# SwiGLU and down projection of a hybrid decoder layer: seven block products in place of eight

## The chip, the cores and the metric

The kernel runs on one NeuronCore of a Trainium2 chip. The metric is the time of one execution on the device in microseconds. TensorE (PE) multiplies matrices and adds up in PSUM; VectorE (DVE), ScalarE (ACT) and GpSimd (POOL) do the elementwise work, the last of them on SBUF alone; SyncE (SP) issues most DMA transfers. Each engine works through its own list of instructions in order and waits on semaphores for the others.

## The reference, cut to what matters

One layer of a decoder trunk over 520 tokens (512 of a prompt, 8 single decode steps), 1024 features wide, all in float32. Two attention mixers come first; the change leaves them alone. Then:

```python
x = x + m @ w_o
gu = _rmsnorm(x, norm2_g) @ w_gu                                     # 1024 -> 2 x 2816
y = x + (jax.nn.silu(gu[..., :D_FF]) * gu[..., D_FF:]) @ w_down      # 2816 -> 1024
```

A last RMSNorm follows. The results are y and the windows of keys and values.

## The kernel before

Activations lie with features on the 128 partitions and tokens along the free axis: 8 chunks of 128 features, each 520 wide, cut in two halves of 256 and 264 tokens. A float32 product is made from three fast ones: each operand is split into a rounded part `hi` and a rest `lo`, and every product is hi·hi + hi·lo + lo·hi, all three into one PSUM bank. So one 128 x 128 block of weights against one half of the tokens is three matmuls (lines 245, 246, 248).

**Weights** come as jobs in a fixed list. SP loads a block of 128 x 1024 values (`raw`, 512 KB); ACT copies it rounded to `whi` (line 137) and DVE subtracts to get `wlo` (line 138). `weights` runs this one job ahead, with three raw buffers.

**SwiGLU** (lines 1152 to 1182): 22 chunks of 128 gated features. A chunk is 8 x 3 x 2 matmuls for the gate, into `psg`, and as many for the up part, into `psu`, so 96. `gated` then takes the SiLU on ACT, multiplies on DVE, copies rounded on ACT and subtracts on DVE: all 22 chunks stay in SBUF as `g_hi` and `g_lo`. The first two chunks run half by half, because the second half of the norm is still being made.

**Down projection** (lines 1264 on): 8 chunks of 128 output features, each 22 x 3 x 2 = 132 matmuls into `psd`, whose bank DVE adds to the residual `x2`. Each finished chunk is transposed to tokens, squared and multiplied with the final gain (`finish`); `emit_last` does the last chunk, the roots and the writes.

GpSimd has next to nothing to do in these two stages. It works in the earlier ones, where it multiplies projections with the rotary tables (lines 387, 428) beside DVE. The order of instructions on each engine is settled when the kernel is built, by the framework's scheduler, which starts from the order of the code; it may move an instruction ahead of others on its engine where no data stand against it. Buffers are waited for as the pools hand them out.

## Time and profile before

| | |
|---|---|
| median of 3 runs (lowest, highest) | 911.19 us (909.94, 915.88) |
| span of the profiled execution | 910.4 us, mean granted clock 0.991 |
| PE busy | 883.6 us, 97% of the span |
| DVE, ACT, POOL busy | 453.2, 340.4, 138.8 us |
| last matmul of the down projection starts | 900.61 us |

The profiled execution's own time is its span, 910.4 us; it lies 0.8 us under the median. The page gives the busy time of each engine, the span in 40 slices, the DMA queues, the chain of work that ended last, and the costliest groups of instructions. A busy PE counts matmuls that overlap in its pipeline, so a matmul's price is read from how many start in a window, not from the duration of one. In a timeline a row is start, duration, engine, line, operation and tiles.

### The profile page before, as it was taken

The numbers are of one execution on the slowest core, as the hardware profiler recorded it, in microseconds if no ns is written. First come the engines' busy times: TensorE is split into PE (matmuls) and PEld (weight loads), VectorE is DVE, ScalarE is ACT, GpSimd is POOL, SyncE is SP. The second block draws the span as 40 slices with busy tenths as digits, with TensorE's granted clock in tenths as the row PEclk, the third lists the DMA queues.
The fourth block names the chain that finished last, engine by engine and source line by source line (L and its number), as shares of the span: only waits on it lengthen the run. The fifth ranks groups of instructions, "written<-read, shape, count | busy, mean of one in ns | idle before, by whom it ended". The sixth has DMA issues, their size and how long they took to land.

```text
span 910.4 us, 17130 instructions
## 1 busy us (share of the span) xinstructions
PE 883.6 (97%) x7104; PEld 833.4 (92%) x7104; DVE 453.2 (50%) x920; ACT 340.4 (37%) x750; POOL 138.8 (15%) x114
## 2 busy tenths in 40 slices
PE   6998989999999999999999999999999999999996
PEld 6898889878998788779999999999999999999995
DVE  4878648754597554724464653333333333233322
ACT  6324324444466655533233443222222222222222
POOL 2335553423232112100000200000000000000000
PEclk9999999999999999999999999999999999999998
DMA  9546745331332211488568339357356555657302
GB/s 298 174 129 189 216 147 181 100 99 47 94 117 94 72 32 60 124 195 233 157 208 272 93 114 278 113 184 229 114 177 194 155 167 174 194 162 235 90 19 95
DMA packets 149854, 137.09 MB, mean 151 GB/s; under 512 B 5344, under 2 KB 144768, under 8 KB 148368
## 3 DMA queue, kind: packets, MB, share of 16 engines
q1 hardware_dynamic: 145472, 83.65, 33.0%
q10 hardware_dynamic: 2592, 46.08, 14.7%
q0 software_dynamic: 1712, 6.26, 2.1%
q8 instruction: 56, 0.92, 0.4%
q14 instruction: 22, 0.18, 0.1%
HBM read 129.14 MB, written 51.86 MB: 199 GB/s over the span
## 4 chain that ended last, share of the span: by engine, by line
PE 83%; DMA 6%; DVE 5%; issue 3%; POOL 2%; ACT 1%; SPq 0%; POOLq 0%; DVEq 0%; ACTq 0%
PE psu L246 5%; PE psu L248 5%; PE psg L248 5%; PE psu L245 5%; PE psg L246 5%; PE psg L245 5%; PE psd L245 4%; PE psd L248 4%; PE psd L246 4%; PE poa L931 3%; DMA raw_wo<-in_w_o 2%; DMA qc<-q_dram 2%; PE psgb L248 2%; PE psgb L245 2%; PE psgb L246 2%
## 5 line engine op out<-in xcount | busy, mean ns | idle before, releaser
L245 PE MATMUL psd<-g_hi,whi_wd 128*128 128x256 f32 (+1 forms) x352 | 93.4, 285 | 0.5 <-DVE x L1266 0.5
L246 PE MATMUL psd<-g_lo,whi_wd 128*128 128x256 f32 (+1 forms) x352 | 93.1, 282 | 0.0
L246 PE MATMUL psu<-h_lo,whi_wu 128*128 128x256 f32 (+1 forms) x352 | 93.0, 283 | 0.0
L246 PE MATMUL psg<-h_lo,whi_wg 128*128 128x256 f32 (+1 forms) x352 | 92.6, 282 | 0.0
L245 PE MATMUL psu<-h_hi,whi_wu 128*128 128x256 f32 (+1 forms) x352 | 92.1, 282 | 0.0
L245 PE MATMUL psg<-h_hi,whi_wg 128*128 128x256 f32 (+1 forms) x352 | 91.6, 282 | 0.0
L248 PE MATMUL psd<-g_hi,wlo_wd 128*128 128x256 f32 (+1 forms) x352 | 74.5, 283 | 0.0
L248 PE MATMUL psu<-h_hi,wlo_wu 128*128 128x256 f32 (+1 forms) x352 | 73.5, 283 | 0.0
L248 PE MATMUL psg<-h_hi,wlo_wg 128*128 128x256 f32 (+1 forms) x352 | 73.4, 282 | 0.0
L245 PEld LDWEIGHTS psd<-g_hi,whi_wd 128*128 128x128 f32 x352 | 66.3, 188 | 0.8 <-DVE x L1266 0.7
L245 PEld LDWEIGHTS psu<-h_hi,whi_wu 128*128 128x128 f32 x352 | 66.3, 188 | 0.0
L246 PEld LDWEIGHTS psd<-g_lo,whi_wd 128*128 128x128 f32 x352 | 66.2, 188 | 0.0
L245 PEld LDWEIGHTS psg<-h_hi,whi_wg 128*128 128x128 f32 x352 | 66.1, 188 | 0.0
L246 PEld LDWEIGHTS psu<-h_lo,whi_wu 128*128 128x128 f32 x352 | 66.1, 188 | 0.0
L246 PEld LDWEIGHTS psg<-h_lo,whi_wg 128*128 128x128 f32 x352 | 66.1, 188 | 0.0
L138 DVE TENSOR_TENSOR wlo_wg<-raw_wg,whi_wg 128x1024 fp32r<-128x1024 f32 x22 | 27.0, 1225 | 74.4 <-ACT whi_wg L137 69.8
L248 PEld LDWEIGHTS psd<-g_hi,wlo_wd 128*128 128x128 f32 x352 | 55.9, 188 | 0.0
L138 DVE TENSOR_TENSOR wlo_wd<-raw_wd,whi_wd 128x1024 fp32r<-128x1024 f32 (+1 forms) x24 | 27.3, 1137 | 57.1 <-ACT whi_wd L137 56.2
L248 PEld LDWEIGHTS psu<-h_hi,wlo_wu 128*128 128x128 f32 x352 | 55.6, 188 | 0.0
L248 PEld LDWEIGHTS psg<-h_hi,wlo_wg 128*128 128x128 f32 x352 | 55.6, 188 | 0.0
L137 ACT ACTIVATE whi_wd<-raw_wd 128x1024 fp32r<-128x1024 f32 (+1 forms) x24 | 23.7, 989 | 84.6 <-PE psd L246 67.9
L1156 DVE TENSOR_TENSOR sg<-sg,psu 128x256 f32<-128x256 f32 (+1 forms) x44 | 16.9, 421 | 72.5 <-PE psu L248 72.5
(371 smaller groups left out, 2465.6 us busy)
## 6 DMA issues: line engine op xcount, KB each, us to landing
raw_wg<-in_w_gu SPq DMA_DIRECT2D x22, 512.0 KB, 3.9
raw_wu<-in_w_gu SPq DMA_DIRECT2D x22, 512.0 KB, 5.3
raw_wd<-in_w_down SPq DMA_DIRECT2D x16, 512.0 KB, 5.5
out<-in_cache_b_kv ACTq DMA_DIRECT2D x8, 1022.0 KB, 5.5
out<-in_cache_b_kv ACTq DMA_DIRECT2D x8, 512.0 KB, 4.0
raw_qa<-in_w_in SPq DMA_DIRECT2D x8, 512.0 KB, 3.8
raw_ga<-in_w_in SPq DMA_DIRECT2D x8, 512.0 KB, 4.8
raw_gb<-in_w_in SPq DMA_DIRECT2D x8, 512.0 KB, 3.9
```

The source lines that it names most:

```text
L137: a = nc.scalar.activation(hi[:, :kc], raw[:, :kc], AF.Copy)
L138: nc.vector.tensor_tensor(lo[:, :kc], raw[:, :kc], hi[:, :kc].bitcast(F32), op=ALU.subtract)
L245: nc.tensor.matmul(ps[i], hi[:, k], xh[:, k0 + k, sl], start=st, stop=False)
L246: nc.tensor.matmul(ps[i], hi[:, k], xl[:, k0 + k, sl], start=False, stop=False)
L248: last_mm[0] = nc.tensor.matmul(ps[i], lo[:, k], xh[:, k0 + k, sl], start=False, stop=en).ins
L931: nc.tensor.matmul(po[64 * kv:64 * kv + 64, :], va[:, j - 1 + r, 64 * kv:64 * kv + 64], pts_[kv, r], start=(r == rel[0]), stop=(r == 1), s ...
L1156: nc.vector.tensor_tensor(sg, sg, pu, op=ALU.mult)
```

## The change

The last two stages become 2 x 2 block products in the form with seven multiplications (Strassen's, with Winograd's sums). Tokens are cut into two halves of 260. Feature chunks go in pairs, an even and an odd one, so the normalised input has four quarters (`hq`, split as `hb_hi`/`hb_lo`), and four sums of quarters are made and split once (`ht_hi`/`ht_lo`, in `sums`). A unit of kind "h" makes the gate and the up part of one chunk of gated features: its 2 x 2 block of weights is gate and up against even and odd. A unit of kind "d" makes two chunks of the output from one group of gated features. Each unit runs seven products q1 to q7 of four pairs each (three in the last group), with three matmuls a pair.

The sums of weight blocks are made on GpSimd in `prepare` (`s`, and `a21` in place), each of the seven operands is split by ACT and DVE as before, and the results are put together from four PSUM tiles (`a`, `e`, `f`, `b`) by DVE, ACT and GpSimd in `run`, `gated` and `down`. Operands are prepared four steps ahead (`NLA`). The first two chunks stay as they were, in `classical`.

Gated features no longer stay for all 22 chunks. Each pair is split, with its sums, as soon as it is made (`split_pair`), and the down projection takes them in three groups of 4, 4 and 3 pairs; so the order is chunks 0 to 8, down 0, chunks 9 to 16, down 1, chunks 17 to 21, down 2. `x2` gathers the three. The output projection and the norm before it get the same halves of 260. Counted from 0, the chunk of the output finished last is number 6, not 7, and `emit_last` and `emit_part` follow that.

On VectorE, the list of two SwiGLU chunks read before (`sg` the gated product, `g_lo` its rest, `wlo_wu` and `wlo_wd` rests of weights):

```order
L1156 TENSOR_TENSOR sg_8273<-sg_8273,psu_8161 128x256
L1156 TENSOR_TENSOR sg_8278<-sg_8278,psu_8162 128x264
L138 TENSOR_TENSOR wlo_wu_8411<-raw_wu_0_8286,whi_wu_8410 128x1024
L1158 TENSOR_TENSOR g_lo<-sg_8273,g_hi 128x256
L1158 TENSOR_TENSOR g_lo<-sg_8278,g_hi 128x264
```

and VectorE's list around units 11 to 13 now (`wlo_u..` rests of operands, `su` a weight sum, `zu` and `zsu` the working tiles of the combination, `psb`, `psa`, `psf` PSUM, `t`, `gb_lo`, `gt_lo` sums and rests of a pair of gated chunks):

```order
L1332 TENSOR_TENSOR zu_7993<-psb_u_8052,zsu_7992 128x260
L1301 TENSOR_TENSOR wlo_u13q_8091<-su_8085,whi_u13q_8090 128x512
L1348 TENSOR_TENSOR zu_7863<-psa_u_7861,zu_7863 128x260
L1301 TENSOR_TENSOR wlo_u13q_8048<-raw_u_7967,whi_u13q_8047 128x512
L1341 TENSOR_TENSOR zsu_7992<-psb_u_8052,zsu_7992 128x260
L1301 TENSOR_TENSOR wlo_u13q_8048<-su_7945,whi_u13q_8047 128x512
L1342 TENSOR_TENSOR zu_7993<-zsu_7992,psa_u_7991 128x260
L1220 TENSOR_TENSOR t_8029<-gq_7730,t_8029 128x260
L1343 TENSOR_TENSOR zsu_7992<-zsu_7992,psf_u_8071 128x260
L1254 TENSOR_TENSOR gb_lo_7751<-gq_7730,gb_hi_7750 128x3x260
```

Two whole-block subtractions per chunk have become seven of half a block, between them the five that read a PSUM bank and those for the pair of gated chunks.

On GpSimd, this is all that its list held before from the norm to the end (`rt`, `fst` and `fpart` are roots, `yts` the final gain):

```order
L1130 TENSOR_TENSOR h_lo<-h2f_5682,h_hi 128x256
L1118 TENSOR_TENSOR rt_5839<-rt_5839,nhalf 128x3
L1186 DMA yts<-in_final_norm_g 128x1024
L1227 TENSOR_TENSOR fst_9880<-fst_9880,nhalf 128x2
L1255 TENSOR_TENSOR fpart<-fpart,nhalf 128x3
```

and this is its list now around units 9 to 12 (`su` and `raw_u` weight sums, `gq` gated chunks, `t` their sums):

```order
L1289 TENSOR_TENSOR su_7669<-su_7669,raw_u_7562 128x512
L1346 TENSOR_TENSOR gq_6936<-gq_6936,zsu_7587 128x260
L1286 TENSOR_TENSOR su_7813<-su_7812,raw_u_7690 128x512
L1350 TENSOR_TENSOR gq_6936<-gq_6936,zu_7588 128x260
L1220 TENSOR_TENSOR t_7756<-gq_6936 128x260
L1285 TENSOR_TENSOR su_7944<-raw_u_7838 128x512
L1289 TENSOR_TENSOR su_7813<-su_7813,raw_u_7690 128x512
L1220 TENSOR_TENSOR t_7756<-gq_6936,t_7756 128x260
L1287 TENSOR_TENSOR raw_u_7838<-raw_u_7836,raw_u_7838 128x4x128
```

An engine that had no elementwise work in these stages now has seven instructions in each unit, all of them reading and writing SBUF.

The diff, cut to its core:

```diff
+NCL = 2
+NLA = 4
+STEP_RATE = 0.2
...
-    for i in range(NF):
+    for i in range(NCL):
         jobs.append((f"wg{i}", NK, [load_plain(cols_of(w_gu[0], P * i), NK)], split_plain))
-        jobs.append((f"wu{i}", NK, [load_plain(cols_of(w_gu[0], DFF + P * i), NK)], split_ff))
-    for i in range(NK):
-        for k0 in (0, 8, 16):
-            kc = min(8, NF - k0)
-            jobs.append((f"wd{i}_{k0}", kc, [load_plain(w_down[0, k0 * P:(k0 + kc) * P, P * i:P * i + P], kc)], split_ff if (i * 3 + k0 // 8) % 2 else split_plain))
+        jobs.append((f"wu{i}", NK, [load_plain(cols_of(w_gu[0], DFF + P * i), NK)], split_cl))
...
+    QOF = {(0, 0): 0, (1, 0): 1, (1, 1): 2, (0, 1): 3}
+    hq = op2.tile([P, 4, 4, HH], F32, tag="opT", name="hq")
+    hb_hi = hm.tile([P, 4, 4, HH], F32R, tag="hm", name="hb_hi")
+    hb_lo = hm.tile([P, 4, 4, HH], F32R, tag="hm", name="hb_lo")
+    pools["cl"] = op2.tile([P, 2 * NCL, NK, P], F32R, tag="opT", name="wcl")
...
+            q, i = QOF[m % 2, h], m // 2
+            nc.vector.scalar_tensor_tensor(hq[:, q, i], x2[:, m, sl], g2[:, m:m + 1], bc, op0=ALU.mult, op1=ALU.mult)
+            nc.scalar.activation(hb_hi[:, q, i], hq[:, q, i], AF.Copy)
+            (nc.gpsimd if h == 0 and m % 2 else nc.vector).tensor_tensor(hb_lo[:, q, i], hq[:, q, i], hb_hi[:, q, i].bitcast(F32), op=ALU.subtract)
...
-    def gated(m, h, pg, pu):
-        sl = slice(*SPAN[h])
-        sg = work.tile([P, HT], F32, tag="z", name=f"sg{m}{h}")[:, :SPAN[h][1] - SPAN[h][0]]
-        nc.scalar.activation(sg, pg, AF.Silu)
-        nc.vector.tensor_tensor(sg, sg, pu, op=ALU.mult)
-        nc.scalar.activation(g_hi[:, m, sl], sg, AF.Copy)
-        nc.vector.tensor_tensor(g_lo[:, m, sl], sg, g_hi[:, m, sl].bitcast(F32), op=ALU.subtract)
...
-    for m in range(2, NF):
-        pgs, pus = pair(f"psg{m}", "m"), pair(f"psu{m}", "b")
-        project(pgs, weights(f"wg{m}"), NK, h2_hi, h2_lo)
-        project(pus, weights(f"wu{m}"), NK, h2_hi, h2_lo)
-        for h in range(2):
-            gated(m, h, pgs[h], pus[h])
...
+    for m in range(NCL):
+        classical(m, 0)
+    for _ in norms[1]:
+        pass
+    mid.close()
...
+    TQ = {"q4": 0, "q5": 1, "q6": 2, "q7": 3}
+    BQ = {"q1": 0, "q2": 1, "q3": 2}
+    trickle = []
+    def sums(b, th, tl, i, engines):
+        t = ffp.tile([P, 4, HH], F32, tag="t", name=f"t{nsum[0]}")
+        nsum[0] += 1
+        def op(e, o, x, y, f):
+            return lambda: engines[e].tensor_tensor(t[:, o], x, y, op=f)
+        return [op(0, 1, b[:, 0], b[:, 3], ALU.subtract), op(1, 3, b[:, 3], b[:, 2], ALU.subtract),
+                op(2, 2, b[:, 2], t[:, 1], ALU.add), op(3, 0, b[:, 1], t[:, 2], ALU.subtract),
+                lambda: nc.scalar.activation(th[:, :, i], t, AF.Copy),
+                lambda: nc.vector.tensor_tensor(tl[:, :, i], t, th[:, :, i].bitcast(F32), op=ALU.subtract)]
+    nsum = [0]
+    ht_hi = op3.tile([P, 4, 4, HH], F32R, tag="opT", name="ht_hi")
+    ht_lo = op3.tile([P, 4, 4, HH], F32R, tag="opT", name="ht_lo")
+    for i in range(4):
+        for f in sums(hq[:, :, i], ht_hi, ht_lo, i, (nc.vector, nc.gpsimd, nc.vector, nc.gpsimd)):
+            f()
...
+    GROUPS = ((0, 4), (4, 4), (8, 3))
+    ops_of = {"h": (hb_hi, hb_lo, ht_hi, ht_lo)}
...
+    def split_pair(n):
+        j = min(n // 4, 2)
+        i = n - GROUPS[j][0]
+        b = gq.pop(n)
+        def parts():
+            bh, bl, th, tl = group_ops(j)
+            nc.scalar.activation(bh[:, :, i], b[:, :3], AF.Copy)
+            nc.vector.tensor_tensor(bl[:, :, i], b[:, :3], bh[:, :, i].bitcast(F32), op=ALU.subtract)
+            trickle[:0] = sums(b, th, tl, i, (nc.vector, nc.gpsimd, nc.vector, nc.gpsimd))
+        trickle.append(parts)
...
+        def prepare(self, q):
+            (a11, a12), (a21, a22) = ((r[:, 0], r[:, 1]) for r in self.raw)
+            if q == "q5":
+                self.s = [ffp.tile([P, 4, P], F32, tag="s", name=f"s{self.name}{e}", bufs=2)[:, :self.np] for e in range(2)]
+                nc.gpsimd.tensor_tensor(self.s[0], a21, a22, op=ALU.add)
+                nc.gpsimd.tensor_tensor(self.s[1], self.s[0], a11, op=ALU.add)
+                nc.gpsimd.tensor_tensor(a21, a11, a21, op=ALU.add)
+            if q == "q3":
+                nc.gpsimd.tensor_tensor(self.s[1], self.s[1], a12, op=ALU.add)
+            src = {"q1": a11, "q2": a12, "q4": a22, "q7": a21}.get(q)
+            if src is None:
+                src = self.s[0 if q == "q5" else 1]
+            e = n_op[0] % 2
+            if e == 0:
+                pool = ffp if n_op[0] // 2 % 3 == 2 else wp
+                n = 1 if pool is ffp else 2
+                op_pair[:] = [pool.tile([P, NK, P], F32R, tag=t, name=f"{t}_{self.name}{q}", bufs=n) for t in ("whi", "wlo")]
+            n_op[0] += 1
+            hi, lo = (t[:, 4 * e:4 * e + self.np] for t in op_pair)
+            a = nc.scalar.activation(hi, src, AF.Copy)
+            nc.vector.tensor_tensor(lo, src, hi.bitcast(F32), op=ALU.subtract)
+            issue_copy(a, STEP_RATE)
+            self.w[q] = (hi, lo)
...
+        def product(self, q, ps, start):
+            hi, lo = self.w.pop(q)
+            bh, bl, th, tl = ops_of[self.kind if self.kind == "h" else self.n]
+            xh, xl, j = (th, tl, TQ[q]) if q in TQ else (bh, bl, BQ[q])
+            for i in range(self.np):
+                first, end = start and i == 0, i == self.np - 1
+                nc.tensor.matmul(ps, hi[:, i], xh[:, j, i], start=first, stop=False, skip_group_check=True)
+                nc.tensor.matmul(ps, hi[:, i], xl[:, j, i], start=False, stop=False, skip_group_check=True)
+                nc.tensor.matmul(ps, lo[:, i], xh[:, j, i], start=False, stop=end, skip_group_check=True)
...
+            self.product(q, {"q1": self.a, "q2": self.a, "q3": self.e, "q5": self.e}.get(q, None) if q in ("q1", "q2", "q3", "q5")
+                         else self.f if q == "q4" else self.b, q in ("q1", "q4", "q5", "q6"))
+            if q == "q1":
+                nc.scalar.activation(self.s1, self.a, AF.Copy)
+            if q == "q6":
+                tt(self.v, self.b, self.s1, op=sub)
...
+        def gated(self, q, tt, sub, add):
+            if q == "q1" and self.n % 2 == 0:
+                new_gq(self.n // 2)
+            g = gq[self.n // 2]
+            g0, g1 = (g[:, QOF[self.n % 2, h]] for h in range(2))
+            if q == "q7":
+                tt(self.u, self.b, self.s1, op=sub)
+                tt(self.c22, self.u, self.e, op=sub)
+                tt(self.u, self.u, self.f, op=add)
+            if q == "q2":
+                nc.scalar.activation(g0, self.a, AF.Silu)
+                nc.gpsimd.tensor_tensor(g0, g0, self.u, op=ALU.mult)
+            if q == "q3":
+                tt(self.v, self.e, self.v, op=sub)
+                nc.scalar.activation(g1, self.v, AF.Silu)
+                nc.gpsimd.tensor_tensor(g1, g1, self.c22, op=ALU.mult)
+                if self.n % 2:
+                    split_pair(self.n // 2)
+        def down(self, q, tt, sub, add):
+            xa, xb = x2[:, 2 * self.p], x2[:, 2 * self.p + 1]
+            h0, h1 = slice(0, HH), slice(HH, T)
+            if q == "q6":
+                nc.gpsimd.tensor_tensor(xa[:, h1], xa[:, h1], self.v, op=sub)
+            if q == "q4":
+                tt(xb[:, h0], xb[:, h0], self.f, op=add)
+            if q == "q7":
+                tt(self.u, self.b, self.s1, op=sub)
+                tt(xb[:, h1], xb[:, h1], self.e, op=sub)
+                xv = xb.rearrange("p (h t) -> p h t", h=2)
+                nc.gpsimd.tensor_tensor(xv, xv, self.u.unsqueeze(1).to_broadcast([P, 2, HH]), op=add)
+            if q == "q2":
+                tt(xa[:, h0], xa[:, h0], self.a, op=add)
+            if q == "q3":
+                tt(xa[:, h1], xa[:, h1], self.e, op=add)
...
+    units = [Unit("h", n) for n in range(NCL, 9)] + [Unit("d", 0, p) for p in range(4)]
+    units += [Unit("h", n) for n in range(9, 17)] + [Unit("d", 1, p) for p in range(4)]
+    units += [Unit("h", n) for n in range(17, NF)] + [Unit("d", 2, p) for p in range(4)]
+    steps_ = []
+    for n, u in enumerate(units):
+        before = [(units[n - 1], "q3")] if n else []
+        late_first = (u.kind, u.n, u.p) == ("d", 2, 0)
+        steps_ += (before + [(u, "q1")] if late_first else [(u, "q1")] + before) + [(u, q) for q in ("q5", "q6", "q4", "q7", "q2")]
+    steps_.append((units[-1], "q3"))
...
+            load_units(units.index(u) + (1 if q in ("q1", "q3", "q5") else 2))
+            u.prepare(q)
+            prepared[0] += 1
...
-    PIECES = ((0, 8), (8, 8), (16, NF - 16))
-    for m in range(NK):
-        pds = pair(f"psd{m}", "m")
-        if m < NK - 1:
-            for k0, kc in PIECES:
-                project(pds, weights(f"wd{m}_{k0}"), kc, g_hi, g_lo, k0=k0, first=k0 == 0, last=k0 + kc == NF)
...
+    ending = []
+    for n, (u, q) in enumerate(steps_):
+        prepare_to(n + 1 + NLA)
+        if u.kind == "d" and q == "q1" and u.p == 0:
+            while trickle:
+                trickle.pop(0)()
+        u.run(q)
+        if u.kind == "d" and u.n == 2:
+            if q == "q1" and u.p == 0:
+                start_final()
+            if q == "q7":
+                ending += [lambda m=2 * u.p + 1: finish(m, (1, 2, 3, 4)), lambda m=2 * u.p + 1: finish(m, (0,))]
+            if q == "q2" and u.p == 3:
+                ending += [lambda: finish(ML, (1, 2)), emit_part, lambda: emit((1, 2))]
+            if q == "q3" and u.p < 3:
+                ending += [lambda m=2 * u.p: finish(m, (1, 2, 3, 4)), lambda m=2 * u.p: finish(m, (0,))]
+        for _ in range(2):
+            if trickle:
+                trickle.pop(0)()
+        if ending and q not in ("q7",) and not (u.kind == "d" and u.n == 2 and u.p == 3 and q == "q2"):
+            ending.pop(0)()
+    for f in ending:
+        f()
     emit_last()
```

More of the change, by code (lines that the diff above doesn't have):

```diff
@@ L1187, in trunk_kernel, with classical @@
[L1187 to L1207 removed]
+    def classical(m, h):
+        pg, pu = banks(f"psg{m}{h}")[h], bank(f"psu{m}{h}")
+        project_q(pg, wgu[m][0], h)
+        if h == 0 and (m, 0) in NORM_AT:
+            next(norms[1], None)
+        project_q(pu, wgu[m][1], h)
+        if h == 0 and (m, 1) in NORM_AT:
+            next(norms[1], None)
+        g = gq[m // 2][:, QOF[m % 2, h]]
+        nc.scalar.activation(g, pg, AF.Silu)
+        nc.vector.tensor_tensor(g, g, pu, op=ALU.mult)
@@ new lines, in trunk_kernel, with yt_of, start_final @@
+    split_pair(0)
+    fin_t = {}
+    def yt_of(j):
+        return fin_t["s"][:NS, 0] if j == 0 else fin_t["p"][:, j - 1]
+    tok = [(NP, NS)] + [(P * j, P) for j in range(4)]
+    ssq = fin.tile([P, 5, NK], F32, name="ssq")
+    ML = NK - 2
+    def start_final():
+        fin_t["p"] = op2.tile([P, 4, D], F32, tag="opT", name="ytp")
+        fin_t["s"] = op2.tile([P, 2, D], F32, tag="opT", name="yts")
+        nc.gpsimd.dma_start(fin_t["s"][:, 1], final_g.unsqueeze(0).to_broadcast([P, D]))
```

217 lines of the change are left out of this document (123 added, 94 removed).

## The prediction

> **What bounds the kernel now.** I read the page's first two parts, for which engine is full and where:
>
> ```profile
> PE 883.6 (97%) x7104; PEld 833.4 (92%) x7104; DVE 453.2 (50%) x920; ACT 340.4 (37%) x750; POOL 138.8 (15%) x114
> PE   6998989999999999999999999999999999999996
> POOL 2335553423232112100000200000000000000000
> PEclk9999999999999999999999999999999999999998
> ```
>
> From the middle of the span to its end TensorE never rests and GpSimd never works. For the price of a matmul I read a window that holds nothing but SwiGLU, and for where it ends the last matmul and the last add:
>
> ```profile
> core 0: us, PE busy (x) PEld busy (x) DVE busy (x) ACT busy (x) POOL busy (x), PEclk, DMA share, GB/s
> 550.00:750.00 200.00, 200.00 (x1669) 200.00 (x1668) 68.80 (x107) 57.68 (x105) 0.00 (x0) 1.00 0.58 175
> ...
> 900.61 0.28 PE L248 MATMUL psd<-g_hi,wlo_wd 128*128 128x264 f32 x1
> 900.93 0.43 DVE L1266 TENSOR_TENSOR x<-x,psd 128x264 f32<-128x264 f32 x1 [1.63 <-PE psd L248]
> ```
>
> 200 / 1669 is 0.1198 us a matmul, at the full clock. DVE is busy 34% there, ACT 29%. So this stage is bounded by the number of matmuls, and DVE and ACT have room.
>
> **What it removes.** A SwiGLU chunk goes from 96 matmuls to 84; 20 chunks change, so 240 fewer. Down goes from 8 x 132 = 1056 to 8 x 84 + 4 x 63 = 924, so 132 fewer. 372 x 0.1198 = 44.6 us. I compare the stretch from the end of the first two chunks' first halves to the last `psd` matmul: 3168 - 96 = 3072 matmuls, 368.0 us, before; 2604 + 96 = 2700, 323.5 us, after. The halves of 260 in place of 256 and 264 leave the columns as they were: nothing.
>
> **What it adds, engine by engine.** The rows that price it:
>
> ```profile
> L138 DVE TENSOR_TENSOR wlo_wg<-raw_wg,whi_wg 128x1024 fp32r<-128x1024 f32 x22 | 27.0, 1225 | 74.4 <-ACT whi_wg L137 69.8 <-PE psg L246 4.6
> L138 DVE TENSOR_TENSOR wlo_wd<-raw_wd,whi_wd 128x768 fp32r<-128x768 f32 x8 | 7.7, 959 | 21.4 <-ACT whi_wd L137 21.4
> L1156 DVE TENSOR_TENSOR sg<-sg,psu 128x256 f32<-128x256 f32 x22 | 9.3, 421 | 72.5 <-PE psu L248 72.5
> L137 ACT ACTIVATE whi_wg<-raw_wg 128x1024 fp32r<-128x1024 f32 x22 | 23.3, 1061 | 77.9 <-PE psg L246 73.4 <-DMA raw_wg<-in_w_gu 4.6
> L137 ACT ACTIVATE whi_wd<-raw_wd 128x768 fp32r<-128x768 f32 x8 | 6.8, 845 | 18.8 <-PE psd L246 14.7 <-PE psg L246 4.1
> L158 POOL TENSOR_TENSOR wlo_qb<-raw_qb,whi_qb 128x512 fp32r<-128x512 f32 x4 | 5.1, 1295 | 9.9 <-ACT whi_qb L157 9.9
> 513.06 0.74 POOL L1130 TENSOR_TENSOR h_lo<-h2f,h_hi 128x256 fp32r<-128x256 f32 x1 [1.04 <-ACT h_hi L1129]
> 513.12 0.47 DVE L1128 SCALAR_TENSOR_TENSOR h2f<-x,g,psr 128x256 f32<-128x256 f32 x1
> ```
>
> Per element DVE takes (1225 - 959) / 256 = 1.04 ns, ACT 0.84, POOL (1295 - 740) / 256 = 2.17; the rest follows by these lines. In the stretch:
>
> - GpSimd: 112 sums of 512 elements (28 units x 4) at 1.30, 16 of 384 at 1.02, 82 of 260 (30 sums of quarters, 40 products of the gate, 12 adds) at 0.75, 12 adds of 520 at 1.31: 145 + 16 + 62 + 16 = 239 us.
> - DVE with both inputs in SBUF: 196 rests of 512 at 0.69, 28 of 384 at 0.56, 30 sums of 260 at 0.43, 15 rests of 1040 at 1.24, 11 of 780 at 0.97: 135 + 16 + 13 + 19 + 11 = 194 us.
> - DVE with a PSUM input: 20 x 5 + 12 x 6 = 172 of 260 at 0.43, or 0.37 from start to start (their ends overlap by some 0.06, as the rows of a timeline do): 64 us. With the 37 final products, DVE holds some 270 us.
> - ACT: 196 roundings at 0.63, 28 at 0.52, 11 at 0.86, 15 at 1.08, 72 of 260 at about 0.4, 37 squares: about 210 us.
>
> Each engine for itself stays under TensorE's 323.5 us. Whether they may be taken each for itself is what decides. The trace has one place where DVE and GpSimd both always had something to do, the first rotary products:
>
> ```profile
> 34.27 1.33 POOL L387 TENSOR_TENSOR cos<-cos,spread 128x520 f32<-128x520 f32 x1
> 35.67 3.37 POOL L428 TENSOR_TENSOR z_qb<-z_qb,cos 128x520 f32<-128x520 f32 x2
> 34.36 1.80 DVE L158 TENSOR_TENSOR wlo_qb<-raw_qb,whi_qb 128x512 fp32r<-128x512 f32 x1 [0.34 <-ACT whi_qb L157]
> 36.08 3.53 DVE L429 TENSOR_TENSOR zs_qb<-zs_qb,sin 128x520 f32<-128x520 f32 x2
> 39.53 0.68 DVE L158 TENSOR_TENSOR wlo_qb<-raw_qb,whi_qb 128x512 fp32r<-128x512 f32 x1
> ```
>
> The same subtraction that takes 0.68 us alone takes 1.80 beside GpSimd, and it ends at 36.16, 0.56 after GpSimd's first product (35.60). From there to the end of GpSimd's third (39.04) lie two of each, 3.44 us, so 1.72 a pair: they take turns, one whole instruction each. Of a turn DVE has 0.56 and GpSimd 1.16; only the start of one lies under the end of the other (alone they take 0.70 and 1.31 by the lines above). The rows at 513 show the other side: a DVE instruction that reads PSUM and one SBUF tile runs 0.47 us right under a GpSimd one, and neither is longer.
>
> The Trainium skill (SBUF — State Buffer, "Who interferes with whom") has the rule that speaks against this change: a VectorE instruction with two SBUF inputs and a GpSimd one that reads SBUF exclude each other for the whole instruction. The turns above agree. Taken to the letter, whole durations in line, it would make a pair 1.31 + 0.70 = 2.01 us by the rows, where 1.72 is measured, so it would give the sum of the third rival.
>
> So the two lists share one thing. With the turns' prices (DVE 0.55 for 512, GpSimd 1.14, the others by the slopes):
>
> - GpSimd: 112 x 1.14 + 16 x 0.87 + 82 x 0.60 + 12 x 1.16 = 204.7 us.
> - DVE: 196 x 0.55 + 28 x 0.42 + 30 x 0.29 + 15 x 1.10 + 11 x 0.83 = 153.9 us.
>
> Together 358.6 us, 35 more than TensorE needs and 9.4 less than the stretch takes now. A single unit of kind "h": GpSimd 4 x 1.14 + 3 x 0.60, DVE 7 x 0.55 and half of 2.51 for the pair, 11.5 us against 84 x 0.1198 = 10.1 on TensorE.
>
> That sum needs GpSimd to run under every DVE instruction that reads PSUM. In DVE's list those stand between the others, so DVE's own line is 153.9 + 64 + 8 (final products) + what of GpSimd's 204.7 is not under the 72: 358.6 if all is, 430 if none. GpSimd mostly has something queued, so I take three quarters, 0.75 x 72 = 54: **376.6 us**.
>
> **New waits.** q7 adds into the bank that q6 filled, so TensorE waits until DVE has read it; behind that wait stand q2 and the next unit's q1 on TensorE, and everything that DVE will make of them. q4 lies between, 12 x 0.1198 = 1.4 us, which covers DVE's 0.43, but not DVE standing behind one GpSimd sum (1.14) and one of its own rests (0.55). The same holds for q3, which waits for the read of `e`. I cost these at nothing beyond the sum above, since they only pass DVE's lateness on; on GpSimd the products of the gate wait for ACT's SiLU, with the next weight sums queued behind them, and that is part of the lost cover.
>
> **Ends of the stretch.** When the last group of gated chunks is ready its last pair must still be gated, split and summed, in a chain over DVE, ACT and POOL of about 0.43 + 0.4 + 0.75 + 0.86 + 0.97 before TensorE can go on, while operands are prepared at most a few steps ahead: I take 3 us (0 to 6). After the last product (1.1 us of nine matmuls) come DVE's subtraction, GpSimd's add over 520, the transposes of seven blocks, and per block a square and a product in turn, 0.7 us each by these rows:
>
> ```profile
> 895.88 0.28 ACT L1205 ACTIVATE sqy<-ty 128x128 f32<-128x128 f32 x1 [5.98 <-PE ty L1201]
> 896.60 0.28 ACT L1205 ACTIVATE sqy<-ty 128x128 f32<-128x128 f32 x1 [0.36 <-DVE ytp L1206]
> 902.93 0.85 POOL L1255 TENSOR_TENSOR fpart<-fpart,nhalf 128x3 f32<-128x3 f32 x1 [4.55 <-DVE fpart L1253]
> 906.09 0.30 SPq L1262 DMA_DIRECT2D out<-yts  x1
> ```
>
> Now the last chunk's add ends at 901.36 and the last write is issued at 906.1, with 4.3 us to the end. In the change some 5 us of blocks and 1 us of the other half's roots come ahead of that: 6 us more (3 to 9). What hides this today is the matmuls of the last half, which no longer come after it.
>
> Nothing else moves the end. Transfers: two 512 KB loads a unit as before, 0.58 of the DMA share now. Copies of state rows: 64, issued within the steps. SP only issues loads, and waits for raw buffers that free one unit ahead. The clock: the page's slices show it at 9 tenths or more also where TensorE is busy 6 to 8 tenths, so gaps of this size cost no clock.
>
> **Sum.** 910.4 - 368.0 + 376.6 + 3 + 6 = 928.0 us of span. The runs' median lies 0.8 above the profiled execution: **928.8**, say 929.
>
> **Rivals.**
> 1. *TensorE stays the bound* (faster). For it: each engine alone fits, and prepared operands lie up to four steps ahead. Against it: all of the sums and rests read SBUF, and the turns at 34 us. It would give 910.4 - 44.6 + 3 + 6 + 4 (the first sums of quarters not hidden) + 0.8 = 880.
> 2. *Perfect turns* (no change). DVE's PSUM work all lies under GpSimd's, so 358.6: 910.4 - 368.0 + 358.6 + 9 + 0.8 = 911.
> 3. *No cover* (slower still). DVE stands whenever GpSimd works, and every step of TensorE stands behind DVE: 430, so 982; with half the cover 946. It decides once GpSimd's queue runs dry while DVE reads PSUM, which its waits for the gate's SiLU could bring about in each unit.
> 4. *The change removes fewer matmuls than it says.* The lists show 2604 and 192; nothing is left for this.
>
> **Chances.** The forecast, 920 to 955: 0.46. Perfect turns, within 1% (902 to 920; a change of 1% is about what this kernel's runs can tell): 0.24. TensorE bound, about 880: 0.20. Little cover, over 955: 0.10. Faster by over 1%: 0.20, within: 0.24, slower: 0.56. Slower is likeliest because the sum of turns lies within 10 us of what it replaces even when nothing is lost, while the ends add 9 us and any lost cover adds more. The forecast's own range is 920 to 955; the range for 8 in 10 takes in the perfect turns and half of the TensorE-bound case, 880 to 958.
>
> **What would show it.** If I am right, the changed profile has TensorE with gaps in every unit and some 11.5 to 12.5 us from one unit to the next; GpSimd and DVE together near full, with rests of 512 well over 0.69 us and sums of 512 over 1.30 on the mean; matmuls waiting for `wlo` rests and for `zu`/`zsu`. If TensorE is still at 1669 matmuls in 200 us there, with rests at 0.69, the turns do not bind and rival 1 holds. If DVE's rests are stretched but TensorE has no gaps, the sum is right and the cover better than I took. I would be wrong about the ends if more than 17 us pass from the last matmul of a product to the end.

## The result, and the profile after

The changed kernel takes 978.5 us (median of 4 runs, 975.1 to 981.6) where the kernel before, on the same chip, takes 913.5 (909.9 to 917.4): a ratio of 1.070, 95% interval 1.065 to 1.076. By the ratio that is 64 us slower, where 929 us, 18 slower, was forecast. The profiled execution has a span of 973.3 us and a mean granted TensorE clock of 0.961; before they were 910.4 and 0.991.

The page of the kernel after, its first two parts (busy time and share of each engine; busy tenths in 40 slices):

```profile
PE 881.9 (91%) x6736; PEld 813.2 (84%) x6736; DVE 687.6 (71%) x1214; ACT 424.7 (44%) x926; POOL 435.6 (45%) x336
PE   7998999999999999999989798879898889899783
POOL 2435624332331121000003568657778777778641
PEclk9999999799999999999999899889999999999796
```

There are 368 matmul records fewer, and yet the span is 63 us longer: TensorE now has gaps from the middle of the span on, in just the slices in which GpSimd is busy. The windows of 40 us show it with the clock (the columns are stretch, busy time and instructions of PE, PEld, DVE, ACT, POOL, granted clock, DMA share, GB/s):

```profile
560.00:600.00 40.00, 34.88 (x266) 33.10 (x264) 35.40 (x44) 18.99 (x36) 29.59 (x21) 0.97 0.56 175
...
720.00:760.00 40.00, 33.04 (x256) 30.95 (x255) 35.96 (x42) 18.48 (x34) 33.61 (x25) 1.00 0.46 142
...
880.00:920.00 40.00, 33.46 (x226) 31.10 (x226) 33.68 (x46) 17.70 (x33) 29.43 (x25) 0.87 0.21 60
```

226 to 266 matmuls in 40 us; at 0.1198 us each 334 fit. DVE and GpSimd together have 63 to 70 us of instructions in flight in 40. Why, the groups and a piece of the timeline show (weight sums on GpSimd, weight rests on DVE, and a DVE instruction that reads PSUM):

```profile
L1287 POOL TENSOR_TENSOR raw_u<-raw_u,raw_u 128x512 f32<-128x512 f32 x19 | 32.3, 1702 | 0.8 <-DMA raw_u<-in_w_gu 0.2
L1301 DVE TENSOR_TENSOR wlo_u17q<-raw_u,whi_u17q 128x512 fp32r<-128x512 f32 x5 | 7.8, 1594 | 0.1
L1332 DVE TENSOR_TENSOR zu<-psb_u,zsu 128x260 f32<-128x260 f32 x20 | 8.4, 419 | 2.3 <-PE psb_u L1313 2.1
```

```profile
743.58 1.74 POOL L1285 TENSOR_TENSOR su<-raw_u 128x512 f32<-128x512 f32 x1
744.09 3.48 DVE L1301 TENSOR_TENSOR wlo_u13q<-raw_u,whi_u13q 128x512 fp32r<-128x512 f32 x2
745.28 1.73 POOL L1289 TENSOR_TENSOR su<-su,raw_u 128x512 f32<-128x512 f32 x1
746.99 1.73 POOL L1287 TENSOR_TENSOR raw_u<-raw_u,raw_u 128x512 f32<-128x512 f32 x1
```

Sum and rest alternate. Each takes 1.73 us, and from one sum's start to the next pass 1.71, for the 1.72 us a pair that the prediction read at 34 us of the trace before. The instruction that reads PSUM is as short as it was (0.42). So the turns are there, at their price. What the prediction priced far too low are the hand-overs between stages. The windows of 5 us around the hand-over to the last group of down products, and the matmul that waited there:

```profile
901.00:906.00 5.00, 1.09 (x7) 0.68 (x6) 4.97 (x6) 1.70 (x4) 5.00 (x6) 1.00 0.00 0
906.00:911.00 5.00, 3.68 (x12) 2.88 (x13) 3.48 (x5) 1.91 (x3) 2.65 (x3) 0.59 0.55 157
911.00:916.00 5.00, 4.42 (x19) 3.82 (x18) 2.92 (x6) 2.52 (x4) 0.41 (x2) 0.50 0.01 2
```

```profile
906.78 0.52 PE L1311 MATMUL psb_d<-gt_hi,whi_d20q 128*128 128x260 f32 x1 [4.33 <-ACT gt_hi L1224]
...
955.15 0.28 PE L1313 MATMUL psb_d<-gt_hi,wlo_d23q 128*128 128x260 f32 x1
955.98 1.28 POOL L1365 TENSOR_TENSOR x<-x,zsd 128x520 f32<-128x520 f32 x1 [2.65 <-DVE zsd L1362]
```

38 matmuls in 15 us, 4.6 us by price: first TensorE stands 4.33 us for the sums of the last group, then the clock is at half. The tiles of these sums are the ones that held the sums of the normed quarters (`group_ops` takes them from the same two buffers), so none can be written before unit 21 has read those: the last matmul that reads `ht` starts at 896.19 and the group's first `gt_hi` at 896.39, though its sums were ready at 873.5. The first down group has such a place too, which the prediction did not name; TensorE waits 3.74 us there, and in the 10 us around it the clock is at 0.63 to 0.69:

```profile
651.15 0.59 PE L1311 MATMUL psa_d<-gt_hi,whi_d00q 128*128 128x260 f32 x1 [3.74 <-ACT gt_hi L1224]
649.00:654.00 5.00, 2.59 (x10) 2.29 (x11) 2.87 (x4) 2.99 (x5) 4.72 (x5) 0.69 0.61 210
654.00:659.00 5.00, 4.81 (x27) 4.51 (x27) 4.75 (x8) 1.21 (x4) 2.32 (x4) 0.63 0.38 105
```

And from the last product's end (955.4) to the end of the span 17.9 us pass; before, from 900.9 to 910.4, 9.5.

The stage by its parts, from the first matmul of each part to the first of the next, in us. "Price" is matmuls x 0.1198, "turns" the prediction's prices by unit (11.5 for SwiGLU; 4 x 1.14 + 0.60 + 1.16 + 7 x 0.55 = 10.2 for down, 8.2 in the last group). The other 15 us of the prediction's 358.6 are the sums and rests of the normed quarters (11.5) and of the first pair (3.7); some 9 of them run after 544.4, in the first row's time. The two columns on the right are experiments that follow.

| part | price | turns | after | no_sums | no_rests |
|---|---|---|---|---|---|
| units 2 to 8 | 70 | 81 | 94 | 78 | 76 |
| first down group | 40 | 41 | 55 | 43 | 43 |
| units 9 to 16 | 81 | 92 | 99 | 85 | 80 |
| second down group | 40 | 41 | 50 | 43 | 42 |
| units 17 to 21 | 50 | 57 | 54 | 52 | 49 |
| last group | 30 | 33 | 59 | 54 | 54 |
| sum | 312 | 344 | 411 | 355 | 343 |
| last product to the end | | | 17.9 | 18.2 | 18.2 |

### The profile page after: what moved, and what is told of

It is laid out like the page before. It is cut to its first block, busy times and chain, and to the rows that moved or that the text cites. A ratio compares the mean times of both kernels' runs of the same rounds, so it can differ in the third digit from the quotient of the medians.

```text
span 973.3 us, 17231 instructions
## 1 busy us (share of the span) xinstructions
PE 881.9 (91%) x6736; PEld 813.2 (84%) x6736; DVE 687.6 (71%) x1214; ACT 424.7 (44%) x926; POOL 435.6 (45%) x336
## 4 chain that ended last, share of the span: by engine, by line
PE 52%; DVE 21%; DMA 9%; POOL 7%; issue 6%; ACT 4%; SPq 0%; DVEq 0%; POOLq 0%; ACTq 0%
PE poa L937 3%; DMA raw_d<-in_w_down 2%; DMA raw_wo<-in_w_o 2%; PE psa_u L1313 2%; PE psa_u L1311 2%; DMA qc<-q_dram 2%; PE psa_u L1312 2%; PE psqa L251 2%; PE psgb L251 2%; PE psgb L254 2%; PE psgb L252 2%; PE psqa L252 2%; PE pspa L252 2%; PE pspa L254 2%; PE psqa L254 2%
## 5 line engine op out<-in xcount | busy, mean ns | idle before, releaser
L251 PE MATMUL pso<-m_hi,whi_wo 128*128 128x260 f32 x128 | 35.8, 290 | 2.9 <-DVE x L1101 2.9
L1286 POOL TENSOR_TENSOR su<-su,raw_u 128x512 f32<-128x512 f32 x20 | 30.0, 1498 | 15.8 <-DVE wlo_u9q L1301 4.8
L251 PE MATMUL psqa<-h_hi,whi_qa 128*128 128x256 f32 (+1 forms) x128 | 35.9, 300 | 0.0
L252 PE MATMUL pso<-m_lo,whi_wo 128*128 128x260 f32 x128 | 35.6, 287 | 0.0
L252 PE MATMUL psqa<-h_lo,whi_qa 128*128 128x256 f32 (+1 forms) x128 | 35.4, 295 | 0.0
L1285 POOL TENSOR_TENSOR su<-raw_u 128x512 f32<-128x512 f32 x20 | 30.4, 1520 | 10.9 <-DMA raw_u<-in_w_gu 6.5
L1289 POOL TENSOR_TENSOR su<-su,raw_u 128x512 f32<-128x512 f32 x20 | 31.2, 1560 | 7.1 <-DVE wlo_u17q L1301 1.8
L252 PE MATMUL psgb<-h_lo,whi_gb 128*128 128x256 f32 (+1 forms) x128 | 34.3, 286 | 0.0
L251 PE MATMUL psgb<-h_hi,whi_gb 128*128 128x256 f32 (+1 forms) x128 | 34.3, 287 | 0.0
L252 PE MATMUL psga<-h_lo,whi_ga 128*128 128x256 f32 (+1 forms) x128 | 34.2, 285 | 0.0
L1287 POOL TENSOR_TENSOR raw_u<-raw_u,raw_u 128x512 f32<-128x512 f32 x20 | 33.8, 1690 | 0.8 <-DMA raw_u<-in_w_gu 0.2
L251 PE MATMUL psga<-h_hi,whi_ga 128*128 128x256 f32 (+1 forms) x128 | 33.8, 284 | 0.0
```

The lines of the kernel that those rows point to most:

```text
L251: nc.tensor.matmul(ps[i], hi[:, k], xh[:, k0 + k, sl], start=st, stop=False)
L252: nc.tensor.matmul(ps[i], hi[:, k], xl[:, k0 + k, sl], start=False, stop=False)
L1285: nc.gpsimd.tensor_tensor(self.s[0], a21, a22, op=ALU.add)
L1286: nc.gpsimd.tensor_tensor(self.s[1], self.s[0], a11, op=ALU.add)
L1287: nc.gpsimd.tensor_tensor(a21, a11, a21, op=ALU.add)
L1289: nc.gpsimd.tensor_tensor(self.s[1], self.s[1], a12, op=ALU.add)
```

## The experiments

All ratios are to the kernel before on the same chip, and kernels that were measured on different chips are compared by them; 1% is 9 us. no_sums, memset_sums, no_rests and no_rests_fin leave a part of the arithmetic out, and serve only to take the time apart.

**Do the weight sums do it, and by the port?** Leave them out; or put fills of about the same length in their place, which read nothing:

```diff
-                nc.gpsimd.tensor_tensor(self.s[0], a21, a22, op=ALU.add)
...
-                src = self.s[0 if q == "q5" else 1]
+            src = {"q1": a11, "q2": a12, "q4": a22, "q7": a21, "q5": a21, "q6": a11, "q3": a12}[q]
```

> Leaves out the 128 sums of weight blocks on GpSimd in the seven-product stage (raw blocks stand in their place). Theory 1 (GpSimd and DVE take turns, and the sum of the turns sets the pace): 112 x 1.14 + 16 x 0.87 = 141.6 us of the 358.6 go, 217 are left, far under TensorE's 323.5, so the stretch from the first two chunks to the last product falls from 437.9 to 330-350 us and the time to 875-895 us, with rests of 512 back at about 0.69 us. Theory 2 (late loads of raw weights and hand-overs set the pace; GpSimd's sums only lie in between): the waits for raw blocks stay, 940-975 us.

```diff
-                nc.gpsimd.tensor_tensor(self.s[0], a21, a22, op=ALU.add)
...
+                for o in (self.s[0], self.s[1], a21):
+                    for _ in range(2):
+                        nc.gpsimd.memset(o, 0.01)
```

> Each of the 128 weight sums on GpSimd becomes two fills of the same tile with a constant, which read nothing, and take about as long together (1024 elements took 0.956 us, so 2 x 0.5). GpSimd is as busy and stands at the same places of the order. Theory 1 (the port that both read through): like no_sums, 875-900 us, rests of 512 at about 0.69. Rival (GpSimd is late with its sums because its own list is long, port or not): 940-975 us. Theory 2 (late loads): 940-975 us.

no_sums: 920.7 us, ratio 1.004 (1.001 to 1.008). memset_sums: 929.6, 1.013 (1.007 to 1.018). So leaving the sums out gives back 0.066, 60 us, and fills in their place keep 53 of these. A group of fills, and a piece of the timeline, of memset_sums:

```profile
L1287 POOL MEMSET su<- 128x512 f32 x80 | 41.2, 528 | 20.5 <-DVE wlo_u19q L1302 4.0 <-PE psr L1141 3.8 <-DVE wlo_u11q L1302 2.1
```

```profile
642.37 0.53 POOL L1287 MEMSET raw_d<- 128x512 f32 x1 [2.92 <-DMA raw_d<-in_w_down]
642.45 0.68 DVE L1302 TENSOR_TENSOR wlo_d00q<-raw_d,whi_d00q 128x512 fp32r<-128x512 f32 x1
```

A rest that starts 0.08 us after a fill takes its 0.68 us, where one beside a sum took 1.74. Over all 196 rests of 512 the mean is 1.12 us in the change and 0.77 in both no_sums and memset_sums. GpSimd's place in the order is the same and its busy time (2 x 0.53 for 1.30) nearly so, so it is mostly its reading that costs. Mostly, because a fill of `su` also needs no raw block, where GpSimd stood some 18 us for raw blocks before the sums at L1285 in the change; how much of the 53 us this gives was not separated. The Trainium skill (SBUF — State Buffer, "Who interferes with whom") says that such a VectorE instruction contends with a GpSimd one that reads SBUF, not with one that only writes it; these rows agree. Neither kernel comes to the 875 to 900 expected: without the sums the stage is close to TensorE's price in its middle (323 matmuls in the 40 us from 665) and 24 us over it in the last group, as the table shows.

**Is it enough to take GpSimd out of the weight sums?**

```diff
-                nc.gpsimd.tensor_tensor(self.s[0], a21, a22, op=ALU.add)
+                nc.vector.tensor_tensor(self.s[0], a21, a22, op=ALU.add)
```

(and so the other three.)

> The 128 weight sums move from GpSimd to DVE; nothing is left out. Theory 1: the turns' sum falls by 141.6 and grows by 112 x 0.55 + 16 x 0.42 = 68.3, to 285; DVE's own line is 153.9 + 68.3 + 64 + 8 = 294 plus a quarter to half of GpSimd's other 63, so 310-326, about TensorE's 323.5. The stretch takes 335-360, the time is 880-905 us. Rival (DVE is the engine that is overloaded, and the turns matter little): DVE's list grows by 112 x 0.69, 975-1020 us. Theory 2 (late loads): 955-985 us.

965.8 us, 1.055 (1.051 to 1.058): 14 us better than the change, and 60 above the upper end of what the theory expected. One window over the stage:

```profile
545.00:905.00 360.00, 320.45 (x2429) 305.20 (x2429) 311.28 (x519) 163.90 (x297) 96.39 (x85) 0.96 0.52 160
```

DVE is busy 86% and TensorE has made 2429 matmuls where 3005 fit. Neither is full: each waits for the other, and with less and less slack in DVE's list every wait for a bank or a raw block is passed on. That reading is argued from the busy times, not shown. The mean rest is down to 0.76 us, so the turns are nearly gone, and yet only 14 us come back: the sums that DVE now makes itself, and the operands that wait for them, take the rest. That the sum of an engine's list lies below the bound did not mean that it is hidden; it is the prediction's rival 1 once more, in my own expectation. How much of it is DVE's list and how much is waiting was not separated.

**Do late raw blocks do it?** Five buffers in place of four, the later sums written over raw blocks to make room; and in sums_dve the two loads of a unit in the other order:

```diff
-                pool = ffp if n_raw[0] % 4 == 3 else wp
+                pool = ffp if n_raw[0] % 5 in (2, 4) else wp
...
-                nc.gpsimd.tensor_tensor(self.s[1], self.s[0], a11, op=ALU.add)
-                nc.gpsimd.tensor_tensor(a21, a11, a21, op=ALU.add)
+                nc.gpsimd.tensor_tensor(a21, a11, a21, op=ALU.add)
+                nc.gpsimd.tensor_tensor(a11, self.s[0], a11, op=ALU.add)
```

> Five buffers for raw weight blocks in place of four (the second and third sum are written over a raw block, which gives the room), so that loads are issued half a unit earlier. Theory 1 (turns): the port has the same work, and only what was idle for a load is won: 960-980 us. Theory 2 (late loads): the waits of 5-10 us for raw blocks go, some 40 us, so 930-945 us.

```diff
-            for e in range(2):
+            for e in (1, 0):
```

> sums_dve with the two loads of a unit issued in the other order: the second raw block first, whose buffer comes free two steps sooner. In sums_dve DVE stood 25 us waiting for raw blocks. Theory 2 (late loads set the pace once GpSimd is out of it): 940-955 us. Theory 1 (DVE's own list of some 310-330 us sets it, and a load only shifts where it waits): 958-970 us.

raw5: 992.5 us, 1.082 (1.075 to 1.089), slower than the change. Its sum over `a11` has to wait for the rests of q1 (groups: 3.2 us each behind `wlo_u21q` and `wlo_u3q` on GpSimd), so it is no clean test of the loads. dve_swap: 959.9, 1.046 (1.040 to 1.052), inside the 958 to 970 of the turns and 0.8% better than sums_dve, with intervals that just overlap. In the two profiles the stage takes 396 us both times, so no cost of late blocks is shown.

**Do ACT and DVE wait for each other in the final steps?** Squares first, then products:

```diff
             nc.scalar.activation(sq[:n], tp[:n, P * i:P * i + P], AF.Square, accum_out=ssq[:n, j, m:m + 1])
+        for i, j in enumerate(js):
+            c0, n = tok[j]
             nc.vector.tensor_tensor(yt_of(j)[:, mc], tp[:n, P * i:P * i + P], gf[:n, mc], op=ALU.mult)
```

> In the final step of a chunk all squares of its blocks (ACT) come first and then all products (DVE), in place of square and product block by block, where each engine waits for the other. Theory 1 (in the last group of down products the pace is DVE's: per unit 8 blocks x 0.72 in turns with ACT, 2 x 0.45, 7 rests x 0.56 and 6 adds x 0.41 = 13.1 us, where 13.4 were measured and TensorE needs 7.5): a unit loses 8 x 0.45 = 3.6 us, four units 14, the tail 2: 960-968 us. Rival (the pace there is set by the weight sums on GpSimd and by the loads): at most 4 us, 974-980 us.

976.7 us, 1.063 (1.055 to 1.070): 0.8% better, 7 us and not 16, with intervals that overlap. In the profile the tail is 2.6 us shorter (15.3) and the last group 3. The 3 are mostly one wait: the last unit's `psb` bank comes from the same pool as the tiles `ty` of the final steps, and TensorE stood for it until a product with the gain was done, in the change (first line) and in finish2 (second):

```profile
950.40 0.39 PE L1311 MATMUL psb_d<-gt_hi,whi_d23q 128*128 128x260 f32 x1 [2.37 <-DVE ytp L1429]
956.87 0.39 PE L1311 MATMUL psb_d<-gt_hi,whi_d23q 128*128 128x260 f32 x1 [0.24 <-DVE ytp L1431]
```

So the turns of ACT and DVE are there, but elsewhere in the last group little is gained without them.

**Does TensorE set the pace once there are fewer turns?** Every second SwiGLU unit with eight products (four weight splits, no sums):

```diff
+            self.plain = kind == "h" and n % 2 == 1
...
+        if u.plain:
+            steps_ += [(u, "p0")] + before + [(u, q) for q in ("p1", "p2", "p3")]
+            continue
```

> Every second one of the 20 SwiGLU units is computed with eight products (four weight splits, no weight sums, no differences of banks; gate and up in banks of their own), the others and the down products stay. Theory 1 (turns): two units have about 16 us of turns against 84 + 96 = 180 matmuls, 21.6 us, so TensorE sets the pace again; at no_sums' 1.05 of the matmuls' price 226 us for the 20 units where 247 were measured: 950-962 us. Rival (each seven-product unit loses some 2.5 us by itself, by hand-overs from engine to engine, whatever stands beside it): 10 x 11.8 + 10 x 12.4 = 242 us, 970-978 us.

> Both edits: every second SwiGLU unit with eight products, and squares ahead of products in the final steps. If the two losses lie in different places they add: 958 - 16 = 942, 935-950 us. If one only moves into the other, 950-965 us.

half: 936.7 us, 1.021 (1.016 to 1.027); half_finish2: 932.3, 1.016 (1.011 to 1.021), just under its 935 to 950. With 120 matmuls more, 14.4 us, half is 45 us faster than the change, more than the 16 to 28 expected. Windows of half:

```profile
705.00:745.00 40.00, 40.00 (x336) 40.00 (x335) 26.38 (x37) 17.95 (x34) 20.47 (x16) 1.00 0.58 180
825.00:865.00 40.00, 40.00 (x336) 40.00 (x336) 25.79 (x39) 15.94 (x31) 16.89 (x13) 1.00 0.41 120
```

TensorE is full at the full clock in the middle of the stage: units 9 to 16 take 85.8 us for 720 matmuls, 86.3 by price. So the turns bind by their amount per matmul, as the sum had it, and there a seven-product unit between two others loses nothing. The edit takes the sums, three of seven rests and the differences of banks away together, so it does not tell them apart. At the start, from 545 to 585, there are still only 243 matmuls.

**Where are the rest of the losses?** half_finish2 with other units as the eight-product ones: the even ones; those and the last; that with the last group's add on DVE; every third and the last.

```diff
-            self.plain = kind == "h" and n % 2 == 1
+            self.plain = kind == "h" and n % 2 == 0
+            self.plain = kind == "h" and (n % 2 == 0 or n == 21)
+            self.plain = kind == "h" and (n % 3 == 2 or n == 21)
```

> half_finish2 with the even units as the eight-product ones in place of the odd: the first unit of the stage no longer needs the sums of the normed features' quarters, the last one does seven products again. Theory (the start of the stage loses some 10 us, since those sums are not ready in time and the matmuls after the gap run at 0.215 us each in place of 0.12): 5 to 9 us are won there, up to 4 given back at the last group: 923-930 us. Rival (the start is bound by the turns of the same instructions, which stay): 930-936 us.

> half_even with the last unit eight-product too, so that the last two units need no tile of the quarter sums and these come free for the last group of gated features 20 us sooner; 12 matmuls more. Theory (the hand-over to the last group costs some 7 us, because its quarter sums can only be written once the last seven-product unit has been through TensorE): 917-926 us, 3-8 under half_even. Rival (the last pair's own chain sets it): within 2 us of half_even.

> half_21 with the add over 520 elements at the end of each unit of the last group on DVE in place of GpSimd (1.29 us in the tail against about 0.7). The tail is 1 us shorter and the last group no slower: 1-3 us under half_21. If DVE is what the last group waits for: the same or 2 us above.

> half_21_add with eight products in every third unit and in the last, 8 of 20, in place of 11. Theory 1 (turns): three units have some 27 us of turns against 264 matmuls, 31.6 us, so TensorE still sets the pace: 36 matmuls fewer, 4.3 us: 911-920 us. Rival (two seven-product units in a row already fall behind, as the groups of down products do): 920-930 us.

half_even: 941.8 us, 1.026 (1.022 to 1.030). Units 2 to 4 are 276 matmuls here and go by in 37 us, where half_finish2's 264 take 41: the start did lose some 5 us to the quarter sums. But by the end of unit 8 that is gone (81.5 us, 80.3 in half_finish2), and the whole is slower than either theory had it. From the first matmul of the last group to the end pass 70 us in place of 61, though units 17 to 21 before it are 6.5 shorter; the two down groups before and units 9 to 16 lose 10 more between them. half_21: 938.2, 1.022 (1.016 to 1.027), 65 us from the last group to the end; its interval overlaps with that of half_even, so the hand-over is at most a part of it. half_21_add: 937.3, 1.022 (1.018 to 1.026), no difference. third_add: 928.0, 1.012 (1.008 to 1.015), not the 911 to 920 of the turns but in its rival's range: two seven-product units in a row fall behind. Its units 9 to 16 take 91 us for 696 matmuls, 83 by price.

From third_add on: the down units' weight sums on DVE; the loads swapped where a seven-product unit lies two before; unit 3 with eight products; the eight-product units ahead of each down group.

```diff
+            ve = nc.vector if self.kind == "d" else nc.gpsimd
-                nc.gpsimd.tensor_tensor(self.s[0], a21, a22, op=ALU.add)
+                ve.tensor_tensor(self.s[0], a21, a22, op=ALU.add)
...
+            for e in ((0, 1) if prior.plain else (1, 0)):
...
+            self.plain = kind == "h" and n in (2, 3, 5, 8, 11, 14, 17, 20, 21)
+            self.plain = kind == "h" and n in (2, 3, 6, 8, 11, 14, 16, 19, 21)
```

> third_add with the weight sums of the down units on DVE, those of the SwiGLU units stay on GpSimd. In third_add the three groups of down products took some 46, 52 and 42 us against 40, 40 and 30 by the matmuls' price. Theory 1 (turns, also there): 48 sums at 0.55 in place of 1.14, 28 us less of turns, of which the excess can give back 8-14: ratio 0.997-1.004 to the kernel before. Theory 2 (raw blocks of the down weights come late, turns or not): within 4 us of third_add, ratio 1.008-1.014.

> third_dsum with the second raw block of a unit loaded first where the unit two before it is a seven-product one, whose second block comes free two steps sooner. Theory 2 (late raw blocks): 4-8 us under third_dsum. Theory 1: within 3 us.

> third_swap with the second unit of the stage computed with eight products too, 12 matmuls more. Theory (the quarter sums of the normed features are not ready for the second unit either; the stretch up to the fifth unit took 12 us more than its matmuls): 3-6 us under third_swap. Rival (the start is behind by DVE's and GpSimd's own work, which PE meets a unit later): 0-2 us above.

> The same number of eight-product units as in third_start, but so placed that one stands right before each group of down products (8, 16, 21). Theory (part of each group's loss is the hand-over of the last gated pair, and an eight-product unit, which adds little to the turns, gives time for it): 2-5 us under third_start. Rival (two or three seven-product units in a row between them fall behind as much as is won): within 2 us.

third_dsum: 920.0 us, 1.0045 (1.0005 to 1.0085), 0.7% better than third_add: a little short of what the turns expected and better than late loads would have made it, though the intervals of the two kernels just touch. In the profiles the first two down groups take 37 and 42 us, 41 and 46 in third_add. third_swap 1.0047 (1.0015 to 1.0079), third_start 1.0060 (1.0022 to 1.0098) and third_ends 1.0075 (1.0037 to 1.0113) cannot be told from it; none of the three theories behind them is borne out. No version that does all of the work came under the kernel before; third_dsum has 276 matmuls fewer (33 us) and lies 0.45% above it.

**What holds the rest?** no_sums without the rests as well, so that DVE's list is short and the port nearly free, and that with squares ahead of products:

```diff
-            nc.vector.tensor_tensor(lo, src, hi.bitcast(F32), op=ALU.subtract)
-            self.w[q] = (hi, lo)
+            self.w[q] = (hi, hi)
```

> no_sums that leaves out the 224 weight rests on DVE in the stage too; the third matmul of each three takes the rounded block again. Of the port's work only the gated features', the adds and the products of the gate are left, of DVE's list some 110 us. Theory 1 alone (what is left in no_sums above the matmuls' price is turns or DVE's own line): 880-892 us. Rival (it is hand-over: the quarter sums at the start and before the last group, the final steps in turns of ACT and DVE, the longer tail): 900-915 us.

> no_rests with squares ahead of products in the final steps. If the turns of ACT and DVE in the final steps are what is left in the last group, 10-14 us under no_rests, the tail's 2-3 among them; if the hand-over of the last group's sums is, only the tail's 2-4.

no_rests: 908.0 us, 0.988 (0.983 to 0.994). no_rests_fin: 903.6, 0.983 (0.980 to 0.987). DVE is then busy 129 of 360 us, and still only 11 of the 44.6 us are there. Windows of 4 us of no_rests at the last group, and the matmuls that waited there:

```profile
836.00:840.00 4.00, 3.65 (x31) 3.47 (x30) 2.40 (x4) 2.07 (x4) 0.75 (x1) 1.00 0.36 107
840.00:844.00 4.00, 2.42 (x20) 2.21 (x19) 1.74 (x4) 1.87 (x4) 2.51 (x3) 1.00 0.00 0
844.00:848.00 4.00, 2.32 (x7) 1.52 (x7) 3.42 (x4) 1.57 (x3) 2.76 (x3) 0.71 0.33 98
848.00:852.00 4.00, 2.71 (x11) 2.41 (x12) 1.58 (x2) 1.34 (x2) 0.94 (x1) 0.50 0.00 0
852.00:856.00 4.00, 4.00 (x20) 3.98 (x20) 1.43 (x4) 1.85 (x4) 0.75 (x1) 0.51 0.16 45
856.00:860.00 4.00, 4.00 (x35) 4.00 (x35) 1.06 (x3) 2.09 (x5) 1.31 (x1) 1.00 0.18 53
```

```profile
844.46 0.39 PE L1301 MATMUL psb_d<-gt_hi,whi_d20q 128*128 128x260 f32 x1 [2.04 <-ACT gt_hi L1224]
845.74 0.58 PE L1302 MATMUL psb_d<-gt_lo,whi_d20q 128*128 128x260 f32 x1 [0.77 <-DVE gt_lo L1225]
847.22 0.58 PE L1301 MATMUL psa_d<-gb_hi,whi_d20q 128*128 128x260 f32 x1 [0.24 <-ACT gb_hi L1253]
848.40 0.58 PE L1302 MATMUL psa_d<-gb_lo,whi_d20q 128*128 128x260 f32 x1 [0.60 <-DVE gb_lo L1254]
850.09 0.58 PE L1301 MATMUL psb_d<-gt_hi,whi_d20q 128*128 128x260 f32 x1 [0.90 <-ACT gt_hi L1224]
```

In the 20 us from 836 to 856 there are 89 matmuls, 10.7 us by price. The chain of the last group, sums on DVE and GpSimd, `gt_hi` on ACT, `gt_lo` on DVE, is a cause by itself, with few turns behind it, and the halved clock that follows is by estimate some 4 of the 9 us lost here (busy time by missing clock, 2.32 x 0.29 + 2.71 x 0.50 + 4.00 x 0.49). The time lies in the range of the hand-over theory, above the 880 to 892 of the turns. By the table, no_rests' loss lies mostly in the last group (24 us over the price), then in the tail (9 more than before) and the first units (5). The squares first give 4 back, with intervals that overlap, as the hand-over theory expected.

So the 64 us come apart, by the ratios: 44.6 us of matmuls gained; 60 lost with the weight sums (all but 8 not lost when fills stand in their place); 15 with the rests (no_sums to no_rests); 34 with what is left, by the table mostly the last group, the tail and the start. 60 + 15 + 34 - 44.6 = 64. The three are what each step of leaving out gave, in this order; another order could share them out otherwise.

## Why the prediction was right and wrong

- *TensorE is the bound before, 372 matmuls are 44.6 us*: right; the middle of half runs at 336 matmuls in 40 us.
- *The price of a turn*: right, 1.71 us a pair in the stage for 1.72 foreseen, and memset_sums shows that it comes of reading beside reading. Rival 1, TensorE stays bound, falls by it. The forecast's direction was right, and by this mechanism.
- *The sum of the turns, 358.6 us*: too small by 18. The prediction's stretch starts after the first 96 SwiGLU matmuls, at 530.4 in the trace after, and its last product ends at 955.4: 425.1 us, where 376.6 + 3 = 379.6 were forecast. In 376.3 of them a GpSimd instruction or a DVE one with two SBUF inputs is in flight. Some 3 us of the excess are rests of the norm, which its list left out. What makes up the others was not separated; the prices are those of an alternation without a gap, and an instruction that meets no other takes its full time (0.69 for 0.55).
- *Three quarters cover*: near. DVE's PSUM reads that lie outside those 376 us are another 22.6, for 18 foreseen (54 of 72 covered). Together 399.0. Rival 3, no cover, names 982 us, close to the 978.5 measured, but its condition is not met: over 70% of these reads are covered, so that nearness is chance.
- *New waits cost nothing beyond the sum*: this is the step that failed first. In the remaining 26 us of the stretch neither does anything, while one waits for TensorE, ACT or a raw block, where 3 us were allowed for; no_rests shows such waits with hardly any turns. Of the 26, 9 lie in the last group and 7 in units 2 to 8. The 3.74 us for `gt_hi` at the first down group had no term at all.
- *The last group's hand-over, 3 us (0 to 6)*: too small by far. The last group took 59 us against 33 by turns, and 54 against 30 by price in no_rests, where there are hardly any turns. Units 17 to 21 took 54 for 57, so a few us of it are work put off. I had counted the chain of one pair; the quarter sums of all three pairs are split only then, because their tiles come free so late.
- *The tail, 6 us (3 to 9)*: 8.4, within its bounds, and outside my own mark of 17 us for the whole.
- *Gaps of this size cost no clock*: wrong. I read it from slices of 23 us, where half-clock stretches of 8 us don't show, and passed over the last slice, where the clock stands at 8 tenths with TensorE busy 6. The mean fell from 0.991 to 0.961, and in stretches of 5 us it is 0.50. The parts of the stage that lost clock:

```profile
544.35:638.73 94.38, 79.08 (x567) 74.24 (x566) 80.73 (x99) 41.21 (x75) 65.26 (x48) 0.91 0.47 140
638.73:694.12 55.39, 48.07 (x351) 46.15 (x349) 40.83 (x59) 19.87 (x36) 36.97 (x29) 0.91 0.50 156
896.31:955.43 59.12, 46.24 (x308) 42.12 (x306) 44.70 (x95) 27.92 (x97) 32.47 (x28) 0.88 0.12 36
```

Busy time by missing clock, 79.08 x 0.09 + 48.07 x 0.09 + 46.24 x 0.12, gives 17 us, an estimate; not all of it need be on the path.
- *Loads cost nothing*: neither raw5 nor dve_swap shows otherwise, and neither settles it.

What would show it: gaps in the units, rests and sums stretched (1.12 and 1.52 us on the mean for 512) came out; 11.5 to 12.5 us a unit held for units 9 to 16 (98.6 / 8 = 12.3), not for units 2 to 8 (13.5) nor 17 to 21 (10.7). The span is 973.3 us where 928.0 were forecast, 45.3 more. In the prediction's own terms: the sum 17.7, the cover 4.6, waits and hand-over 23.1, the tail 2.4, less 2.5 by which the stretch starts earlier than forecast.
